# `w_down` by Strassen's seven block products, with weight blocks summed by accumulating DMAs

## The chip, the cores and the metric

The kernel runs on one core of one Trainium2 chip. The core has TensorE (PE), VectorE (DVE), ScalarE (ACT) and GpSimd (POOL), each with a queue of its own that runs in order, and 16 DMA engines; SyncE (SP) issues the transfers. The metric is the device time of one execution in microseconds; the median of three timed runs is shown.

## The reference

One decoder layer over 512 tokens of width 1024 in float32: token mixing (sparse attention beside dilated attention), cross-attention into 256 memory tokens, and the MLP that the change is about:

```python
hm = rmsnorm(x, norm_mlp_g[l])
x = x + jnp.square(jax.nn.relu(hm @ w_up[l])) @ w_down[l]      # w_up 1024 x 4096, w_down 4096 x 1024
return rmsnorm(x, norm_final_g)
```

## The kernel before

Every dense product is done in three passes. A float32 operand is split into `hi`, its value rounded to the type `float32r`, and `lo`, the rest; `mm3` (line 155) issues for each chunk of 128 contracted rows the matmuls hi x hi, hi x lo and lo x hi. All matmuls are issued in line 107. One has a stationary block of 128x128 and moves 512 columns through it.

Weights come in units of two chunks, [128, 2, 512] or 512 KB. `load_weight` (line 132) loads a unit with SP into `wraw` (three buffers), ACT rounds it into `whi` (line 129), and POOL or DVE subtracts to give `wlo` (line 130). `whi` and `wlo` have six buffers each. A string such as "vppp" says for the four units of a load who subtracts: v is DVE, p is POOL.

The MLP is a loop over four quarters `g` of 1024 hidden features (line 782). In each quarter `up_groups` computes the hidden features transposed, features on partitions and 512 tokens in columns, in eight groups of 24 matmuls. `evac_up` takes a group out of its PSUM bank (three banks `mm`): ACT applies relu, DVE squares, ACT rounds to hi and DVE subtracts to lo (lines 800 to 804). Then `project_add` (line 579) multiplies by the quarter's 1024 rows of `w_down`: for two halves of 512 columns and four tiles of 128 tokens, eight chunks by three matmuls; DVE multiplies the bank by the row's 1/rms squared (`r_mlp2`) and adds it to the residual `xr` (line 596). In the last quarter `finish` follows each addition: the row's square sum, 1/rms on POOL, the final gain (half on POOL, line 770), and the stores.

A planner in the compiler orders the instructions of each engine by a simulated time line. While `ordered[0]` is true, PE's instructions keep the order of the program; in the MLP this ends after the first `w_up` half. Tiles of one tag share buffers, and a writer waits for the last reader of the buffer it takes.

Of the kernel before, what the change touches and what calls it, by code (L numbers as in the profile page):

```python
# [17 lines left out]
P = 128  # L18
# [46 lines left out]
def kernel(  # L65
# [89 lines left out]
    def mm3(dst, a, b, first=True, last=True, ks=None):  # L155
        """dst += sum_k a_k^T b_k, a and b as (hi list, lo list); lo x lo is below float32."""
        n = len(a[0])
        for k in ks if ks is not None else range(n):
            mmul(dst, a[0][k], b[0][k], start=first and k == 0, stop=False)
            mmul(dst, a[0][k], b[1][k], start=False, stop=False)  # L160
            mmul(dst, a[1][k], b[0][k], start=False, stop=last and k == n - 1)
# [40 lines left out]
    def transpose_half(rows, g0, his, los, bank=bank_tp):  # L202
        """rows [128 tokens, 4 chunks of 128] -> transposed, times the gain, as hi + lo per chunk."""
# [11 lines left out]
    # =============================== token mixing ===============================  # L215
    p1a, p1b = ExitStack(), ExitStack()
# [267 lines left out]
    def keys_a():  # L484
        """Group A's keys and values from the latents."""
        p1a.close()
        res = state["res"] = ctx.enter_context(tc.tile_pool(name="res", bufs=1, reuse_waits="tile"))
        uv_raw = mtile([P, NH, DH], F32, "wraw", 3)
# [25 lines left out]
        vA = state["vA"] = [res.tile([P, 2, 512], F32, name=f"vA{c}") for c in "ab"]  # L514
# [34 lines left out]
    # dense products, attention and top-k in turns, so that each engine has work from another  # L549
# [21 lines left out]
    p1b.close()  # L571

    p2 = ctx.enter_context(tc.tile_pool(name="tmp2", bufs=1, reuse_waits="tile"))

# [32 lines left out]
    def up_groups(ms, wt, rhs, evac):  # L607
        """Weight-stationary groups: a new phase starts on the K chunks that are whole first."""
# [23 lines left out]
    def half_square(i, t, c0=0, c1=512):  # L632
        """What columns c0..c1 of half i of token tile t add to the row's mean square."""
# [35 lines left out]
    # =============================== cross-attention ===============================  # L669
# [19 lines left out]
    def cross_probs(h):  # L689
        """Head h's softmax over the memory tokens, transposed: per half of the queries (hi, lo)."""  # L690
# [66 lines left out]
    # =============================== squared-ReLU MLP ===============================  # L757
# [5 lines left out]
    r_mlp2 = p2.tile([P, NT], F32, name="r_mlp2")  # L763
    nc.vector.tensor_tensor(r_mlp2, r_mlp, r_mlp, op=ALU.mult)

    def finish(i, t, c0=0, c1=512):
        half_square(i, t, c0, c1)
        lo = xr[t][:, 0:512]
        if i == 0:
            nc.gpsimd.tensor_tensor(lo, lo, g_fin[0], op=ALU.mult)  # L770
# [5 lines left out]
        hi = xr[t][:, 512:]  # L776
        nc.scalar.activation(lo, lo, AF.Copy, scale=r)
        nc.sync.dma_start(out_rows[:, t, 0:512], lo)
        nc.vector.scalar_tensor_tensor(hi, hi, r, g_fin[1], op0=ALU.mult, op1=ALU.mult)
        nc.sync.dma_start(out_rows[:, t, 512:], hi)  # L780

    for g in range(4):
        if g % 2 == 0:
            hh = mtile([P, KD, S], F32R, "h0")
            hl = [mtile([P, 4, S], F32R, f"u2{c}") for c in "ab"]
            hid_hi = [hh[:, k, :] for k in range(KD)]
            hid_lo = [hl[k // 4][:, k % 4, :] for k in range(KD)]
        else:
            hh = [mtile([P, 2, S], F32R, f"ghi{i}") for i in range(4)]
            hl = [mtile([P, 2, S], F32R, f"glo{i}") for i in range(4)]  # L790
            hid_hi = [hh[k // 2][:, k % 2, :] for k in range(KD)]
            hid_lo = [hl[k // 2][:, k % 2, :] for k in range(KD)]
        for i in range(2):
# [15 lines left out]
        def hid(t):  # L809
            tsl = slice(t * P, (t + 1) * P)  # L810
            return [a[:, tsl] for a in hid_hi], [a[:, tsl] for a in hid_lo]

        project_add(w_down[0], 8 * g, hid, finish if g == 3 else None, "vppp", scale=r_mlp2, last=g == 3)


# [27 lines left out]
```

## Time and profile before

| what | value |
|---|---|
| timed runs | 846.23, 846.34, 846.51 us; median 846.34 |
| profiled execution, first to last instruction (span) | 843.6 us |
| median beyond that span | 2.7 us |
| PE busy | 821.7 us, 97% |
| DVE, ACT, POOL busy | 474.4 (56%), 331.4 (39%), 293.2 us (35%) |
| granted PE clock, mean | 0.992 |
| moved by DMA | 77.34 MB, 92 GB/s |

The profile has no other time of the profiled execution than its span, from the first to the last instruction; the timed runs also hold what lies around that. Busy time of PE is that of pipelined matmuls, so the distance from one matmul to the next is read from counts in a stretch and not from the length of one.

### The profile page before, as it was taken

The numbers are of one execution on the slowest core, as the hardware profiler recorded it, in microseconds if no ns is written. First come the engines' busy times: TensorE is split into PE (matmuls) and PEld (weight loads), VectorE is DVE, ScalarE is ACT, GpSimd is POOL, SyncE is SP. The second block draws the span as 40 slices with busy tenths as digits, with TensorE's granted clock in tenths as the row PEclk, the third lists the DMA queues.
The fourth block names the chain that finished last, engine by engine and source line by source line (L and its number), as shares of the span: only waits on it lengthen the run. The fifth ranks groups of instructions, "written<-read, shape, count | busy, mean of one in ns | idle before, by whom it ended". The sixth has DMA issues, their size and how long they took to land.

```text
span 843.6 us, 11086 instructions
## 1 busy us (share of the span) xinstructions
PE 821.7 (97%) x4182; PEld 679.2 (81%) x4182; DVE 474.4 (56%) x1010; ACT 331.4 (39%) x676; POOL 293.2 (35%) x179
## 2 busy tenths in 40 slices
PE   7899999999999999999999999999999999999997
PEld 6788787886787788788898878888888888888886
DVE  7876999998777634535673344423542244225413
ACT  5354424457754524223464433213431243123322
POOL 5734303131513405544501233333333333333351
PEclk9899999999999999999999999999999999999999
DMA  7443122112412303332510223333233322322202
GB/s 278 125 125 88 33 74 70 63 21 80 150 53 99 96 5 100 99 100 86 184 56 19 82 100 101 101 99 100 100 100 99 100 100 97 103 91 85 99 1 100
DMA packets 44516, 77.34 MB, mean 92 GB/s; under 512 B 4752, under 2 KB 10544, under 8 KB 44464
## 3 DMA queue, kind: packets, MB, share of 16 engines
q1 hardware_dynamic: 44464, 76.64, 27.8%
q8 instruction: 33, 0.54, 0.3%
q14 instruction: 19, 0.16, 0.1%
HBM read 74.01 MB, written 2.10 MB: 90 GB/s over the span
## 4 chain that ended last, share of the span: by engine, by line
PE 85%; DVE 11%; issue 1%; POOL 1%; ACT 1%; DMA 0%; SPq 0%; POOLq 0%; ACTq 0%; DVEq 0%
PE mm L107 71%; PE tp L112 5%; PE sc L107 5%; PE pv L107 4%; DVE m L525 1%; DVE ghi L360 1%; DVE tok L279 1%; DVE glo L526 1%; DVE rb L271 1%; DVE tok L271 1%; DVE whi L127 1%; DVE wlo L130 1%; DVE ghi L526 1%; DMA u2a<-in_x_dram 0%; DVE ghi L358 0%
## 5 line engine op out<-in xcount | busy, mean ns | idle before, releaser
L130 POOL TENSOR_TENSOR wlo<-wraw,whi 128x1024 fp32r<-128x1024 f32 (+2 forms) x107 | 256.2, 2408 | 404.5 <-ACT whi L129 318.8
L107 PE MATMUL mm<-whi,h 128*128 128x512 f32 (+2 forms) x624 | 200.1, 381 | 3.9 <-DVE h L213 2.0
L129 ACT CAST whi<-wraw 128x1024 fp32r<-128x1024 f32 (+3 forms) x111 | 114.3, 1030 | 149.6 <-PE mm L107 105.4
L107 PE MATMUL mm<-h,whi 128*128 128x512 f32 (+1 forms) x448 | 154.9, 369 | 0.0
L107 PE MATMUL mm<-wlo,h 128*128 128x512 f32 (+2 forms) x376 | 141.9, 379 | 0.2 <-DVE wlo L130 0.2
L107 PEld LDWEIGHTS mm<-whi,h 128*128 128x128 f32 x624 | 117.9, 195 | 22.0 <-ACT whi L129 2.2
L107 PE MATMUL mm<-u,whi 128*128 128x512 f32 x320 | 124.7, 390 | 0.0
L107 PE MATMUL mm<-u,wlo 128*128 128x512 f32 x320 | 123.5, 389 | 0.0
L107 PE MATMUL mm<-whi,ghi 128*128 128x512 f32 (+1 forms) x264 | 102.0, 390 | 0.0
L107 PE MATMUL mm<-whi,glo 128*128 128x512 f32 (+1 forms) x264 | 101.5, 385 | 0.0
L107 PE MATMUL mm<-wlo,ghi 128*128 128x512 f32 (+1 forms) x264 | 100.7, 383 | 0.0
L107 PEld LDWEIGHTS mm<-h,whi 128*128 128x128 f32 x448 | 81.1, 188 | 14.3 <-issue 1.0
L130 DVE TENSOR_TENSOR wlo<-wraw,whi 128x1024 fp32r<-128x1024 f32 (+2 forms) x24 | 62.2, 2591 | 37.5 <-ACT whi L129 37.5
L107 PEld LDWEIGHTS mm<-wlo,h 128*128 128x128 f32 x376 | 72.6, 194 | 11.1 <-DVE wlo L130 0.6
L107 PEld LDWEIGHTS mm<-u,whi 128*128 128x128 f32 x320 | 60.1, 188 | 12.4
L107 PEld LDWEIGHTS mm<-u,wlo 128*128 128x128 f32 x320 | 60.0, 188 | 12.5
L802 DVE TENSOR_TENSOR sq<-r 128x512 f32<-128x512 f32 x32 | 22.0, 689 | 66.7 <-ACT r L800 66.7
L107 PEld LDWEIGHTS mm<-whi,glo 128*128 128x128 f32 x264 | 49.6, 188 | 10.1 <-issue 0.2
L107 PEld LDWEIGHTS mm<-wlo,ghi 128*128 128x128 f32 x264 | 49.7, 188 | 9.6 <-issue 0.4
L107 PEld LDWEIGHTS mm<-whi,ghi 128*128 128x128 f32 x264 | 49.6, 188 | 9.4 <-issue 0.2
L409 ACT ACTIVATE p<-p,mx 128x128 f32<-128x128 f32 (+3 forms) x64 | 35.8, 560 | 29.4 <-DVE mx L407 28.5
L800 ACT ACTIVATE r<-mm 128x512 f32<-128x512 f32 x32 | 19.1, 598 | 64.8 <-PE mm L107 64.8
(212 smaller groups left out, 1116.7 us busy)
## 6 DMA issues: line engine op xcount, KB each, us to landing
wraw<-in_w_up_dram SPq DMA_DIRECT2D x32, 512.0 KB, 3.8
wraw<-in_w_down_dram SPq DMA_DIRECT2D x32, 512.0 KB, 3.6
wraw<-in_w_in_dram SPq DMA_DIRECT2D x16, 512.0 KB, 3.6
wraw<-in_w_kv_cross_dram SPq DMA_DIRECT2D x16, 512.0 KB, 3.9
wraw<-in_w_out_dram SPq DMA_DIRECT2D x8, 512.0 KB, 3.6
wraw<-in_w_q_cross_dram SPq DMA_DIRECT2D x8, 512.0 KB, 3.6
wraw<-in_w_o_cross_dram SPq DMA_DIRECT2D x8, 512.0 KB, 4.1
wraw<-in_w_in_dram SPq DMA_DIRECT2D x8, 256.0 KB, 2.9
```

Of the source, the lines that this page charges most:

```text
L107: ins = nc.tensor.matmul(*a, **k)
L112: ins = nc.tensor.transpose(*a, **k)
L127: nc.vector.tensor_copy(hi, raw)
L129: nc.scalar.copy(hi, raw)
L130: (nc.gpsimd if how in "pP" else nc.vector).tensor_tensor(lo, raw, f32(hi), op=ALU.subtract)
L271: nc.vector.scalar_tensor_tensor(o, i, r, tab, op0=ALU.mult, op1=ALU.mult)
L279: nc.vector.tensor_tensor(dst[:, :, c, :], ra[:, :, c, :], rbv[:, :, c, :], op=ALU.add)
L360: nc.vector.scalar_tensor_tensor(acc[b], rl[:, :n], wh, acc[b], op0=ALU.mult, op1=ALU.add)
L409: nc.scalar.activation(pr[:, c], pr[:, c], AF.Exp, bias=mx[:, i:i + 1], scale=-1.0, accum_out=sm[:, i:i + 1])
L526: nc.vector.match_replace(acc[b], m8, acc[b], GONE)
L800: nc.scalar.activation(r, ps, AF.Relu)
L802: nc.vector.tensor_tensor(sq, r, r, op=ALU.mult)
```

## The change

Each quarter's product with `w_down` (512 tokens x 1024 features by 1024 x 1024) is seen as 2 x 2 blocks: tokens in halves of 256, features in even and odd chunks of 128, output columns in halves of 512. Seven block products instead of eight are formed by Winograd's variant of Strassen's scheme, each of two token tiles by four chunks by three matmuls. Three kinds of sums belong to it:

- Sums of hidden blocks, `s` with four slots, are made in `evac_up` from each pair of an even and an odd chunk: four DVE operations of 256 columns, one ACT rounding, one subtraction on POOL (on DVE for the last pair).
- Sums of weight blocks are made by DMA: a tile `xw` is loaded with block (1, 0) and POOL then issues transfers with `accum_op=ALU.add` that add blocks (1, 512), (2, 512) and (2, 0) one after the other; after each step the tile is split. One product uses the sum of two blocks loaded in the same way into `wraw`.
- Products are added to or subtracted from the four blocks of `xr`, by DVE from the bank, or by an ACT copy and POOL additions. Two banks (`keep`) gather products 1, 7 and 4 over the quarter, two others (`five`) products 5 and 6.

The row's 1/rms is now multiplied in before the square: `row_scale` transposes it once on PE, and the evacuation is max(ps, 0) x rT on DVE and the square on ACT. `finish` takes the halves of a row in either order. Group A's values `vA` get a pool of their own which is closed before the pool of the later stages is opened. `ordered` stays true through the MLP. Besides, comments are gone.

```diff
+    def weight_pair(w, rows, c0, how, plus=None):
+        raw = mtile([P, 2, 512], F32, "wraw", 3)
+        nc.sync.dma_start(raw, rows(w)[:, :, c0:c0 + 512])
+        if plus is not None:
+            prows, p0 = plus
+            nc.gpsimd.dma_start(raw, prows(w)[:, :, p0:p0 + 512], accum_op=ALU.add)
+        return split_pair(raw, how)
+
+    def split_pair(raw, how):
+        hi = mtile([P, 2, 512], F32R, "whi", 6)
+        lo = mtile([P, 2, 512], F32R, "wlo", 6)
+        split_unit(raw, hi, lo, how)
+        return hi, lo
...
-    r_mlp2 = p2.tile([P, NT], F32, name="r_mlp2")
-    nc.vector.tensor_tensor(r_mlp2, r_mlp, r_mlp, op=ALU.mult)
+    def row_scale():
+        tp = bank_tp()
+        for t in range(NT):
+            tpose(tp[:, t * P:(t + 1) * P], r_mlp[:, t:t + 1].to_broadcast([P, P]), ident)
+        rT = p2.tile([P, S], F32, name="rT")
+        nc.scalar.copy(rT, tp)
+        rows_ready.append(rT)
...
             def evac_up(m, ps, i=i):
+                if not rows_ready:
+                    row_scale()
                 c = 4 * i + m
+                q, odd = c // 2, c % 2
-                nc.scalar.activation(r, ps, AF.Relu)
+                nc.vector.scalar_tensor_tensor(r, ps, 0.0, rows_ready[0], op0=ALU.max, op1=ALU.mult)
-                nc.vector.tensor_tensor(sq, r, r, op=ALU.mult)
-                nc.scalar.copy(hid_hi[c], sq)
-                nc.vector.tensor_tensor(hid_lo[c], sq, f32(hid_hi[c]), op=ALU.subtract)
+                nc.scalar.activation(sq, r, AF.Square)
+                ring[odd] = sq
+                part, src = (slice(1, 3), sq) if odd else (slice(0, 1), sq[:, 0:256])
...
+                nc.scalar.copy(hi, src)
+                nc.vector.tensor_tensor(lo, src, f32(hi), op=ALU.subtract)
+                if not odd:
+                    return
...
+                s = p2.tile([P, 4, 256], F32, name=nm("S"), tag="S", bufs=1)
+                nc.vector.tensor_tensor(s[:, 0], a22, a21, op=ALU.subtract)
+                nc.vector.scalar_tensor_tensor(s[:, 1], s[:, 0], -1.0, a11, op0=ALU.mult, op1=ALU.subtract)
+                nc.vector.tensor_tensor(s[:, 2], a11, a21, op=ALU.subtract)
+                nc.vector.scalar_tensor_tensor(s[:, 3], s[:, 1], -1.0, a12, op0=ALU.mult, op1=ALU.subtract)
+                nc.scalar.copy(s_hi[q], s)
+                (nc.gpsimd if q < 3 else nc.vector).tensor_tensor(s_lo[q], s, f32(s_hi[q]), op=ALU.subtract)
 
             up_groups(list(range(4)), wt, hm, evac_up)
-            ordered[0] = False
...
-        project_add(w_down[0], 8 * g, hid, finish if g == 3 else None, "vppp", scale=r_mlp2, last=g == 3)
+        xw = mtile([P, 2, 2, 512], F32, "u2b")
+        def sums(step):
+            row, col = ((1, 0), (1, 512), (2, 512), (2, 0))[step]
+            out = []
+            for u in range(2):
+                src = unit_rows(g, row, u)(w)[:, :, col:col + 512]
+                if step == 0:
+                    nc.sync.dma_start(xw[:, u], src)
+                else:
+                    nc.gpsimd.dma_start(xw[:, u], src, accum_op=ALU.add)
+                out.append(split_pair(xw[:, u], "p"))
+            return out
...
+        wts = sums(0)
+        for t in range(2):
+            product(keep[t], t, of_a(0), wts)
+            p1 = p2.tile([P, 512], F32, name=nm("p1"), tag="pc", bufs=2)
+            nc.scalar.copy(p1, keep[t])
+            add(t, left, p1, eng=nc.gpsimd)
+        wts = block(2, 0, "vp")
+        for t in range(2):
+            ps = bank_mm()
+            product(ps, t, of_a(1), wts)
+            add(t, left, ps)
+            done(0, t)
+        wts = sums(1)
+        five = [bank_tp() for _ in range(2)]
+        for t in range(2):
+            product(five[t], t, of_s(1), wts)
+            add(t + 2, right, five[t], ALU.subtract)
+        wts = block(2, 512, "vp")
+        for t in range(2):
+            product(five[t], t, of_s(4), wts, first=False)
+            add(t, right, five[t], ALU.subtract)
+        wts = sums(2)
+        for t in range(2):
+            product(keep[t], t, of_s(2), wts, first=False)
+            u2 = p2.tile([P, 512], F32, name=nm("u2"), tag="pcT1", bufs=2)
+            nc.scalar.copy(u2, keep[t])
+            add(t, right, u2, ALU.subtract, nc.gpsimd)
+            add(t + 2, right, u2, ALU.subtract, nc.gpsimd)
+            done(1, t)
+        wts = block(1, 512, "vp", (2, 512))
+        for t in range(2):
+            ps = bank_mm()
+            product(ps, t, of_s(3), wts)
+            add(t + 2, left, ps)
+            add(t + 2, right, ps, ALU.subtract)
+            done(1, t + 2)
+        wts = sums(3)
+        for t in range(2):
+            cuts = (0, 512) if g < 3 or t == 0 else (0, 256, 512)
+            for c0, c1 in zip(cuts, cuts[1:]):
+                product(keep[t], t, of_a(2), wts, first=False, cut=slice(c0, c1))
+                add(t + 2, slice(c0, c1), keep[t][:, c0:c1])
+                done(0, t + 2, c0, c1)
```

## Rows read from the trace of the kernel before

**Rows 1.** Busy us (instructions) of each engine by stretch, MLP stage; last columns clock, DMA share, GB/s.
```profile
core 0: us, PE busy (x) PEld busy (x) DVE busy (x) ACT busy (x) POOL busy (x), PEclk, DMA share, GB/s
520.00:600.00 80.00, 80.00 (x354) 66.25 (x353) 30.21 (x25) 23.20 (x28) 27.11 (x11) 1.00 0.28 92
680.00:760.00 80.00, 80.00 (x354) 66.25 (x353) 31.88 (x26) 24.17 (x29) 29.49 (x12) 1.00 0.31 105
760.00:843.60 83.60, 77.35 (x364) 64.83 (x363) 29.82 (x33) 26.31 (x42) 28.72 (x23) 0.98 0.20 70
```

**Rows 2.** Chain that ended last, from 480 us: start us, us, what.
```profile
490.87 0.70 PE tp L112 x4
491.57 340.05 PE mm L107 x1500
...
831.64 0.76 DVE xr L596
...
832.49 0.73 ACT junk L642 x2
...
833.56 0.55 POOL rfin L182
...
839.07 0.75 DVE xr L779
```

**Rows 3.** Waits from 490 us: who <- for whom: us in total, times, longest.
```profile
POOL wlo L130 <- ACT whi L129: 202.9, 28, 12.7
ACT whi L129 <- PE mm L107: 84.8, 26, 13.4
```

**Rows 4.** The same for the queue of SP, which issues the loads.
```profile
SPq L145 <- POOL wlo L130: 235.0, 28, 14.7
```

**Rows 5.** Instructions of single lines: duration ns min/median/max, first and last start us, shapes.
```profile
L596 DVE SCALAR_TENSOR_TENSOR xr<-mm,r_mlp,xr x17: 479/750/752, 548.8 to 837.4; 128x512 f32<-128x512 f32 x15, 128x256 f32<-128x256 f32 x2
...
L800 ACT ACTIVATE r<-mm x32: 597/598/599, 499.8 to 793.6; 128x512 f32<-128x512 f32 x32
...
L802 DVE TENSOR_TENSOR sq<-r x32: 676/692/693, 500.4 to 796.6; 128x512 f32<-128x512 f32 x32
...
L804 DVE TENSOR_TENSOR u2b<-sq,h x8: 691/693/2486, 519.8 to 710.9; 128x512 fp32r<-128x512 f32 x8
...
L594 DVE TENSOR_TENSOR xr<-xr,mm x8: 671/683/689, 316.0 to 489.9; 128x512 f32<-128x512 f32 x8
...
L130 POOL TENSOR_TENSOR wlo<-wraw,whi x107: 1831/2397/2852, 11.2 to 815.4; 128x1024 fp32r<-128x1024 f32 x98, 128x768 fp32r<-128x768 f32 x8, 128x928 fp32r<-128x928 f32 x1
...
L130 DVE TENSOR_TENSOR wlo<-wraw,whi x24: 833/3118/3415, 8.1 to 793.3; 128x1024 fp32r<-128x1024 f32 x22, 128x928 fp32r<-128x928 f32 x1, 128x512 fp32r<-128x512 f32 x1
...
L770 POOL TENSOR_TENSOR xr<-xr,g_fin x2: 1292/1294/1297, 811.8 to 818.2; 128x512 f32<-128x512 f32 x2
...
L129 ACT CAST whi<-wraw x111: 624/1052/1057, 7.1 to 812.6; 128x1024 fp32r<-128x1024 f32 x100, 128x768 fp32r<-128x768 f32 x8, 128x928 fp32r<-128x928 f32 x2, 128x512 fp32r<-128x512 f32 x1
```

**Rows 6.** Timeline of SP's queue, two stores of a finished tile: start us, us, what.
```profile
826.59 0.36 SPq L778 DMA_DIRECT2D out_dram<-u3a  x1
827.00 0.42 SPq L780 DMA_DIRECT2D out_dram<-u3a  x1
```

**Rows 7.** DMA issues: what, queue, count, KB each, median us to landing.
```profile
wraw<-in_w_down_dram SPq DMA_DIRECT2D x32, 512.0 KB, 3.6
```

**Rows 8.** Timeline of DVE, three los beside POOL: start us, us, what, [idle before].
```profile
703.82 2.49 DVE L804 TENSOR_TENSOR u2b<-sq,h 128x512 fp32r<-128x512 f32 x1 [1.35 <-ACT h L803]
706.23 3.42 DVE L130 TENSOR_TENSOR wlo<-wraw,whi 128x1024 fp32r<-128x1024 f32 x1
...
728.05 3.12 DVE L130 TENSOR_TENSOR wlo<-wraw,whi 128x1024 fp32r<-128x1024 f32 x1 [4.46 <-ACT whi L129]
```

**Rows 9.** Timeline of POOL in the same stretches.
```profile
703.35 5.21 POOL L130 TENSOR_TENSOR wlo<-wraw,whi 128x1024 fp32r<-128x1024 f32 x2 [10.78 <-ACT whi L129]
...
725.34 4.75 POOL L130 TENSOR_TENSOR wlo<-wraw,whi 128x1024 fp32r<-128x1024 f32 x2 [11.02 <-ACT whi L129]
```

More of the change, by code (lines that the diff above doesn't have):

```diff
@@ L153, in load_weight, with mm3 @@
         return his, los
-    def mm3(dst, a, b, first=True, last=True, ks=None):
+    def weight_pair(w, rows, c0, how, plus=None):
[10 more added lines that the diff above has]
+        return hi, lo
+    def mm3(dst, a, b, first=True, last=True, ks=None, again=False):
         n = len(a[0])
         for k in ks if ks is not None else range(n):
-            mmul(dst, a[0][k], b[0][k], start=first and k == 0, stop=False)
-            mmul(dst, a[0][k], b[1][k], start=False, stop=False)
-            mmul(dst, a[1][k], b[0][k], start=False, stop=last and k == n - 1)
+            mmul(dst, a[0][k], b[0][k], start=first and k == 0, stop=False, skip_group_check=again)
+            mmul(dst, a[0][k], b[1][k], start=False, stop=False, skip_group_check=again)
+            mmul(dst, a[1][k], b[0][k], start=False, stop=last and k == n - 1, skip_group_check=again)
     mhalf = main.tile([P, 1], F32, name="mhalf")
@@ L213, in transpose_half @@
                 nc.vector.scalar_tensor_tensor(los[c], tps[i][:, j, :], g, f32(his[c]), op0=ALU.mult, op1=ALU.subtract)
-    p1a, p1b = ExitStack(), ExitStack()
+    p1a, p1b, va_pool = ExitStack(), ExitStack(), ExitStack()
     att = p1b.enter_context(tc.tile_pool(name="att", bufs=1, side="right"))
@@ L487, in keys_a @@
         res = state["res"] = ctx.enter_context(tc.tile_pool(name="res", bufs=1, reuse_waits="tile"))
+        own = va_pool.enter_context(tc.tile_pool(name="va", bufs=1, reuse_waits="tile"))
         uv_raw = mtile([P, NH, DH], F32, "wraw", 3)
@@ L513, in keys_a @@
         nc.sync.dma_start(kA_all[64:96, :, :], krT[64:96, None, :].to_broadcast([32, NH, S]))
-        vA = state["vA"] = [res.tile([P, 2, 512], F32, name=f"vA{c}") for c in "ab"]
+        vA = state["vA"] = [own.tile([P, 2, 512], F32, name=f"vA{c}") for c in "ab"]
         for t in range(NT):
@@ L571 @@
     p1b.close()
+    va_pool.close()
     p2 = ctx.enter_context(tc.tile_pool(name="tmp2", bufs=1, reuse_waits="tile"))
@@ L762 @@
         nc.sync.dma_start(g_fin[h], norm_final_g[:, 512 * h:512 * h + 512].to_broadcast([P, 512]))
-    r_mlp2 = p2.tile([P, NT], F32, name="r_mlp2")
-    nc.vector.tensor_tensor(r_mlp2, r_mlp, r_mlp, op=ALU.mult)
+    rows_ready = []
+    def row_scale():
[5 more added lines that the diff above has]
+        rows_ready.append(rT)
+    ended = {}
     def finish(i, t, c0=0, c1=512):
         half_square(i, t, c0, c1)
-        lo = xr[t][:, 0:512]
-        if i == 0:
-            nc.gpsimd.tensor_tensor(lo, lo, g_fin[0], op=ALU.mult)
+        part = xr[t][:, 512 * i:512 * i + 512]
+        if t not in ended:
+            nc.gpsimd.tensor_tensor(part, part, g_fin[i], op=ALU.mult)
+            ended[t] = i
             return
@@ L775, in finish, with unit_rows @@
         rstd_of(half_ss.pop(t), r)
[L776 to L780, printed above, removed]
-    for g in range(4):
[L783 to L792, printed above, removed]
+        first = xr[t][:, 512 * (1 - i):512 * (1 - i) + 512]
+        nc.scalar.activation(first, first, AF.Copy, scale=r)
+        nc.sync.dma_start(out_rows[:, t, 512 * (1 - i):512 * (1 - i) + 512], first)
+        nc.vector.scalar_tensor_tensor(part, part, r, g_fin[i], op0=ALU.mult, op1=ALU.mult)
+        nc.sync.dma_start(out_rows[:, t, 512 * i:512 * i + 512], part)
+    lo2 = p2.tile([P, 3, 256], F32R, name="lo2")
+    ring = {}
+    def unit_rows(g, row, u):
+        return lambda w: w[8 * P * g:8 * P * (g + 1), :].rearrange("(k q p) c -> p q k c", q=2, p=P)[:, row - 1, 2 * u:2 * u + 2]
+    for g in range(4):
+        big = mtile([P, 5, 3, 256], F32R, "h0")
+        two = mtile([P, 2, 3, 256], F32R, "u2a")
+        a_hi = [big[:, i] for i in range(4)]
+        a_lo = [two[:, 0], two[:, 1], lo2, big[:, 4]]
+        s_hi = [mtile([P, 4, 256], F32R, f"ghi{i}") for i in range(4)]
+        s_lo = [mtile([P, 4, 256], F32R, f"glo{i}") for i in range(4)]
         for i in range(2):
@@ new lines, in evac_up @@
+                ring[odd] = sq
+                part, src = (slice(1, 3), sq) if odd else (slice(0, 1), sq[:, 0:256])
+                hi = a_hi[q][:, part].rearrange("p s t -> p (s t)")
+                lo = a_lo[q][:, part].rearrange("p s t -> p (s t)")
+                nc.scalar.copy(hi, src)
+                nc.vector.tensor_tensor(lo, src, f32(hi), op=ALU.subtract)
+                if not odd:
+                    return
+                a11, a21 = ring[0][:, 0:256], ring[0][:, 256:]
+                a12, a22 = ring[1][:, 0:256], ring[1][:, 256:]
@@ new lines @@
+            up_groups(list(range(4)), wt, hm, evac_up)
+        xw = mtile([P, 2, 2, 512], F32, "u2b")
+        w = w_down[0]
+        def sums(step):
[9 more added lines that the diff above has]
+            return out
@@ new lines, in block, with product @@
+        def block(row, col, how, plus=None):
+            return [weight_pair(w, unit_rows(g, row, u), col, how[u],
+                                None if plus is None else (unit_rows(g, plus[0], u), plus[1])) for u in range(2)]
+        def product(dst, t, a, wts, first=True, cut=slice(0, 512)):
+            his, los = a
+            tsl = slice(t * P, (t + 1) * P)
+            mm3(dst[:, cut], ([h[:, tsl] for h in his], [l[:, tsl] for l in los]),
+                ([wts[k // 2][0][:, k % 2, cut] for k in range(4)], [wts[k // 2][1][:, k % 2, cut] for k in range(4)]),
+                first, again=True)
@@ new lines, in of_a, with of_s, add @@
+        def of_a(slot):
+            return [h[:, slot] for h in a_hi], [l[:, slot] for l in a_lo]
+        def of_s(n):
+            return [h[:, n - 1] for h in s_hi], [l[:, n - 1] for l in s_lo]
+        left, right = slice(0, 512), slice(512, D)
+        def add(t, half, src, op=ALU.add, eng=nc.vector):
+            dst = xr[t][:, half]
+            eng.tensor_tensor(dst, dst, src, op=op)
+        done = finish if g == 3 else lambda i, t, c0=0, c1=512: None
+        keep = [bank_s() for _ in range(2)]
```

2 lines of the change are left out of this document (removed).

## The prediction

> **What bounds the kernel now.** I read the engines' busy time by stretch first. The MLP (every matmul of `w_up` and `w_down`) lies between 491.6 us and the end. In each 80 us of it PE is busy for 80.00 us with 354 matmuls at a granted clock of 1.00, while DVE, ACT and POOL are busy for about 30, 23 and 27 us [rows 1]. The chain of waits says the same: one piece of 340.05 us is matmuls behind one another, 1500 of them [rows 2]. So a matmul of 512 columns costs 80.00 / 354 = 0.226 us of the end time, and whatever the others do is hidden. The list of waits shows why: POOL waits for ACT's rounding, ACT for PE to free a weight buffer [rows 3], SP's loads for POOL [rows 4]. Weights are ready early and stand before PE. What is taken off PE comes off the end, as long as the three others keep up; that is the question here.
>
> **What is removed.** A quarter of `w_down` (1024 hidden features) is 2 halves x 4 token tiles x 8 chunks x 3 = 192 matmuls. Seven products of 2 token tiles x 4 chunks x 3 = 24 make 168. Four quarters: 96 matmuls fewer, 96 x 0.226 = 21.7 us. PE's order is written out for the whole MLP (`ordered` stays true), so no planner can lose this count.
>
> **What is added on PE.** `row_scale` transposes four 128x128 tiles once; four such took 0.70 us [rows 2]: +0.7. Its copy stands before the first evacuations, but three `mm` banks and two more half groups (2 x 12 x 0.226 = 5.4 us) cover 0.6 us of ACT.
>
> **Evacuation.** The 1/rms is now in the first step (DVE, from the bank, like L596's 0.75 us), the square goes to ACT (like L800, 0.60), so a bank is freed by DVE 0.15 us later. A group of 24 matmuls lasts 5.4 us and there are three banks: nothing. If DVE were late by over 10 us, PE would wait.
>
> **DVE and ACT budgets.** A quarter now lasts 360 x 0.226 = 81.4 us. DVE gains 16 operations of 256 columns for S (0.44 each: L802's 0.69 scaled by L596's 0.48 to 0.75) = 7.0, one 1024-wide lo and one more weight lo (up to 3.4 each [rows 5]) = 6.8, and 12 adds of 0.69 for 8 of 0.75 = 2.3; 16 us more than about 30. ACT gains 6 weight roundings and 4 for S (10 x 1.05) and 4 copies of 0.6: 13 more than 24. Both stay under 60% and are hidden.
>
> **POOL's budget decides.** Today it does 12 weight los of 2.4 us a quarter. After: 6 (`w_up`) + 8 (`sums`) + 3 (`block`) = 17, 3 of S, 6 adds of 1.29 (like L770 [rows 5]) and 8 accumulating DMAs of d each: 20 x 2.4 + 7.7 + 8d = 55.7 + 8d of 81.4 us. That fits; its distribution is tight. Let T0 be the first matmul of product 1. A product is 24 x 0.226 = 5.4 us, seven are 38 us. There are 6 weight buffers (`whi`, `wlo`), 2 per product: a buffer is freed about 12 us before its next contents are needed, so POOL can't work ahead. Between T0-3 and T0+42, when the next `w_up` needs its fourth unit, POOL owes 9 los for the products, 3 for `w_up` (28.8 us), 6 adds (7.7) and 6 DMAs (those of `sums(1)` go before T0): 36.5 + 6d. DVE operations that share its reads push it: 3 weight los and the S chain, up to 7.8 us; half is 3.9. Demand 40.4 + 6d, room 44.7: POOL is late by 6d - 4.3.
>
> No DMA is issued from POOL in this trace, so d has ends only: SP's issue of a plain transfer, 0.36 to 0.42 us, and the whole way of 512 KB from issue to landing, 3.6 us [rows 6, 7]. These give no lateness and 17.3 us a quarter, 0 to 69 us in all. I take d = 1.0, an estimate: an issue is of the kind of the first row, and an accumulating one names its destination twice over 256 rows, hence some 2.5 times as much. Lateness 1.7 x 4 quarters = +6.8 us. (The last quarter has no `w_up` behind it, -7.2 us, but four multiplications by the final gain, 4 x 1.29 = 5.2, on the same queue.)
>
> The Trainium skill ("DMA: Bandwidth & Descriptors", Latency and other measured facts) gives a first byte after about 1 us for such DMAs, put down to descriptor emission on POOL's cores, against 0.6 us for SP's. No row here shows it; by it d would be about 1 too, and the sum the same.
>
> **Waits queued on POOL.** An accumulating DMA waits for its tile's previous split, or for SP's load; behind it stand los of the next units and the adds of product 7. Product 3's DVE adds to the same `xr` columns wait for these adds, and `mm` banks behind them; at 1.7 us that is inside the two spare banks.
>
> **DMA.** Bytes for `w_down` double (8 blocks of 1 MB a quarter for 4), 12 MB in 81 us for 8 in 87; the 16 engines were busy 0.28 to 0.31 of the time [rows 1], so 0.30 x 1.6 = 0.48, and with the reading of the destinations, 4 MB more, 0.65. The chain of one `xw` half per step is landing + rounding 1.05 + lo 2.4. `sums(2)` can be issued at about T0+6, once product 5's units are split (buffers free at T0, one rounding, two los); with landing L, `sums(3)` follows at 13 + L (rounding, two los, an issue) and its second lo ends at 16.4 + 2L; product 4 needs it at T0+32.6. So L may be 8.1 us, over twice the plain 3.6: no cost taken.
>
> **Tail and the rest.** The end chain (add, square sum, POOL's power, scaling, store; [rows 2]) is the same with halves swapped: 0. Reusing the memory of `vA` makes the first tiles of the last pool wait for group A's last products, behind which `keys_cross` keeps PE busy: 0.
>
> **Sum**, against the profiled execution: span 843.6 - 21.7 + 0.7 + 6.8 = 829.4 us. The median of the timed runs is 846.3, 2.7 us above that span; the same 2.7 gives 832.1, so 832.
>
> **Rivals.**
> 1. *POOL's queue is the bound (the other side).* If an accumulating DMA costs POOL more than d = 1.6, the lateness 6d - 4.3 exceeds (21.7 - 0.7) / 4 = 5.3 us a quarter and the change loses. At d = 2.2: 8.9 x 4 = 35.6, so 846.3 - 21.0 + 35.6 = 861. For it: no row caps d below 3.6, and the queue is in order. Against: POOL is at 33% now, and an SP issue takes 0.4.
> 2. *DVE behind POOL's reads.* The rows show it: of 512-column los, median 0.69, the one that began inside a POOL lo took 2.49, ending with it; the next took 3.42, and another one 3.12 [rows 5, 8, 9]; the last ended 1.1 us after POOL. After T0, the last hidden chunk goes through DVE 0.75, ACT 0.6 + 0.6, DVE lo, four S operations, ACT 1.05 and DVE's `s_lo`, which product 5's twelfth matmul needs at T0 + 10.9 + 11 x 0.226 = 13.4. If POOL has no gap, six of these wait out a POOL lo each and the last adds its 1.1: 3.0 + 6 x 2.4 + 1.1 = 18.5, 5.1 us late, x 4 = 20.4: 846.3 - 21.0 + 20.4 = 846, no change. For it: POOL's demand after T0. Against: while it issues DMAs (4 us) and waits for landings it reads nothing, and DVE then does several in a row. Behind it stands the Trainium skill ("SBUF — State Buffer", Who interferes with whom): a DVE instruction with two SBUF inputs contends with a POOL instruction that reads SBUF, and the second to issue is blocked to the end of the first. By this rule the trace agrees (2.49 for 0.69), and the sum would be 846.
> 3. *Accumulation is slow.* If a landing takes L over 8.1 us, each further us costs 2 a quarter. At L = 14 (four plain ones): 11.8 x 4 = 47, so 872. Break-even at 8.1 + 5.3 / 2 = 10.8. For it: the destination must be read too. Against: the 16 engines are idle 70% of the time.
>
> **Chances.** Forecast (lateness 0 to 4.3 us a quarter, so 825 to 842): 0.60. Rival 1: 0.17. Rival 2: 0.13, of which 0.05 still faster, 0.05 same, 0.03 slower. Rival 3: 0.10. A measurement of this kernel tells 0.2% (1.7 us) from no change. Faster 0.65, same 0.05, slower 0.30. The likeliest case's own range is 825 to 842; with rivals 1 and 2 the range is 825 (no lateness: 846.3 - 21.0) to 861, leaving out rival 3 and the far end of 1.
>
> **What would show it.** Right: about 96 matmuls fewer; in each 80 us of the MLP PE busy over 76, clock 1.00; POOL 75 to 85% busy in the `w_down` stretches; accumulating DMAs landing within 8 us; PE's few gaps in front of products 6, 7, 3 or 4, ended by POOL's lo. Rival 1: the same gaps with POOL at 100%, and 2 us or more between its instructions around each DMA. Rival 2: gaps before product 5 ended by DVE's `s_lo`. Rival 3: ACT's rounding of `xw` waiting for a DMA, POOL idle. The prediction is wrong if POOL is late by over 5 us a quarter, or if PE's clock falls below 1.00 after such gaps, which no row prices.

## The result, and the profile after

The changed kernel takes 873.2 us (four runs, 871.2 to 876.3) where the kernel before takes 846.4 (four runs): a ratio of 1.0315 (95% interval 1.0292 to 1.0338). The forecast was 832 and its range ended at 861, so both sign and size were wrong. The profiled execution took 871.23 us with a span of 869.5.

The profile of the kernel after, its parts on busy time, queues (packets, MB, share of 16 engines' span) and DMA issues (last column: median us from issue to landing), and the line of one issuing instruction (duration ns min/median/max), show what the change was to do, and what it cost:

```profile
PE 813.1 (94%) x4078; PEld 667.5 (77%) x4078; DVE 553.2 (64%) x1097; ACT 376.4 (43%) x733; POOL 446.5 (51%) x267
...
q0 software_dynamic: 8704, 16.78, 12.0%
...
wraw<-in_w_down_dram SPq DMA_DIRECT2D x24, 512.0 KB, 4.8
u2b<-in_w_down_dram POOLq DMA_DIRECT2D x24, 512.0 KB, 6.5
...
wraw<-in_w_down_dram POOLq DMA_DIRECT2D x8, 512.0 KB, 6.4
...
L881 POOL DMA_DIRECT2D u2b<-in_w_down_dram x24: 1176/1208/2153, 525.5 to 842.6; - x24
```

The queue `q0` is new. It holds the 32 accumulating transfers, and a median one keeps POOL for 1.21 us (`u2b` is the memory of `xw`) and lands 6.4 to 6.5 us after its issue; SP's loads of `w_down` beside them went from 3.6 [rows 7] to 4.8.

By stretch, the MLP stage of the kernel after (columns as in [rows 1]):

```profile
520.00:600.00 80.00, 71.97 (x300) 58.53 (x299) 44.77 (x45) 30.80 (x38) 57.33 (x31) 0.94 0.60 145
600.00:680.00 80.00, 71.34 (x306) 58.25 (x305) 46.35 (x41) 31.73 (x39) 64.06 (x33) 0.96 0.57 134
627.00:676.00 49.00, 40.34 (x169) 32.58 (x168) 26.64 (x21) 16.34 (x19) 40.74 (x23) 0.93 0.64 144
...
636.00:642.00 6.00, 5.66 (x25) 4.64 (x26) 4.26 (x6) 4.38 (x5) 4.90 (x4) 1.00 1.08 189
642.00:647.00 5.00, 5.00 (x24) 4.14 (x23) 0.69 (x1) 0.00 (x0) 1.61 (x1) 1.00 0.95 257
```

Where 354 matmuls ran in 80 us, about 303 do now: PE has gaps in the MLP for the first time. POOL is at 72 to 80%, in the `w_down` stretch of a quarter (627 to 676) at 83%: busy, not full. The last two lines matter most. Over 80 us the 16 DMA engines are busy 0.57 to 0.60 of the time, a little under the 0.65 worked out beforehand; in the eleven microseconds from 636 they are busy all of it (a share can pass 1, as a packet's whole time is counted where it starts).

What PE waits for from 490 us in the kernel after (us in total, times, longest):

```profile
PE tp L107 <- DVE xr L906: 23.5, 4, 7.6
...
PE mm L107 <- DVE h L854: 3.2, 3, 1.1
...
PE sc L107 <- DVE xr L906: 3.1, 1, 3.1
PE sc L107 <- DVE h L854: 3.1, 1, 3.1
```

Four waits, one a quarter, make 23.5 us, and they are for an addition on DVE (L906), not for a weight. All the waits shown, 32.9 us, are for DVE; the one that is left out here for POOL is 0.9 us. The chain of waits through the second quarter's gap tells why (start us, us, what):

```profile
633.23 1.19 POOL u2b L881
...
635.99 10.93 DMA u2b<-in_w_down_dram
...
647.97 1.05 ACT whi L129
...
649.04 5.70 DVE wlo L130
654.74 0.61 DVE xr L906
...
655.40 4.72 PE tp L107 x12
```

Read it backwards. Product 6's second token tile starts at 655.40, because it gathers in the bank that product 5's addition has to read first. That addition could have run from about 645.1, when product 5 was over (647.79 less product 6's first tile, 12 x 0.227), but in DVE's queue it stands behind a subtraction for product 3's first weight unit, a product that comes two later. That subtraction waited for ACT's rounding, and the rounding, whose own transfer was issued at 635.24 and so had landed by 642.1 (the longest of its kind took 6.8 us), stood in ACT's queue behind that of `xw`, which waited for an accumulating DMA that took 10.93 us. So a late transfer whose result PE did not need yet stopped PE through two queues that run in order. The timelines of ACT, of DVE and of POOL in the kernel after show the pieces:

```profile
647.02 1.05 ACT L129 CAST whi<-u2b 128x1024 fp32r<-128x1024 f32 x1 [5.98 <-DMA u2b<-in_w_down_dram]
647.97 1.04 ACT L129 CAST whi<-wraw 128x1024 fp32r<-128x1024 f32 x1
```
```profile
642.39 0.69 DVE L906 TENSOR_TENSOR xr<-xr,tp 128x512 f32<-128x512 f32 x1 [0.41 <-PE tp L107]
649.04 5.70 DVE L130 TENSOR_TENSOR wlo<-wraw,whi 128x1024 fp32r<-128x1024 f32 x1 [5.96 <-ACT whi L129]
```
```profile
633.23 1.19 POOL L881 DMA_DIRECT2D u2b<-in_w_down_dram  x1
...
635.24 1.65 POOL L162 DMA_DIRECT2D wraw<-in_w_down_dram  x1
635.99 2.14 POOL L881 DMA_DIRECT2D u2b<-in_w_down_dram  x1
...
648.56 5.09 POOL L130 TENSOR_TENSOR wlo<-u2b,whi 128x1024 fp32r<-128x1024 f32 x2
```

DVE idles 5.96 us, then its subtraction takes 5.70 us instead of a median 1.226: it began inside two subtractions of POOL and ended 1.1 us after them, the pattern of [rows 8, 9]. PE stopped at 655.40 - 7.61 = 647.79. Of the gap of 7.61 us, 5.70 - 1.23 = 4.5 are this blocking; the other 3.1 would have gone, by this sum, had the transfer landed in 7.8 us instead of 10.93. POOL had issued three accumulating transfers within 3 us while the DMA engines were full.

The gap also costs clock. PE's timeline in the kernel after, from the end of the gap, and the stretches there (the granted clock is the third number from the right):

```profile
655.40 0.80 PE L107 MATMUL tp<-whi,ghi 128*128 128x512 f32 x1 [7.61 <-DVE xr L906]
655.99 0.63 PE L107 MATMUL tp<-wlo,ghi 128*128 128x512 f32 x1
656.41 0.63 PE L107 MATMUL tp<-whi,glo 128*128 128x512 f32 x1
...
```
```profile
655.00:659.00 4.00, 3.60 (x9) 2.87 (x10) 0.94 (x2) 0.00 (x0) 3.37 (x2) 0.50 0.88 156
...
662.00:669.00 7.00, 7.00 (x32) 5.82 (x31) 0.68 (x2) 3.99 (x5) 6.97 (x6) 1.00 0.40 73
```

For some 3.6 us the granted clock is 0.50, the lower of the two levels (1.2 GHz), and matmuls follow each other at 0.43 us, not 0.227. Eight of them cost 8 x 0.20 = 1.6 us more after this gap. Over the whole MLP 52 matmuls stand 0.3 to 0.9 us behind the one before, most of them after a gap, and together they take some 10 us over 0.226 each. With PE's waits that accounts for most of the 45.9 us by which the four quarters exceed their matmuls (below).

### The profile page after: what moved, and what is told of

Its sections match the earlier page's. It is cut to its first block, busy times and chain, and to the rows that moved or that the text cites. A ratio compares the mean times of both kernels' runs of the same rounds, so it can differ in the third digit from the quotient of the medians.

```text
span 869.5 us, 11165 instructions
## 1 busy us (share of the span) xinstructions
PE 813.1 (94%) x4078; PEld 667.5 (77%) x4078; DVE 553.2 (64%) x1097; ACT 376.4 (43%) x733; POOL 446.5 (51%) x267
## 3 DMA queue, kind: packets, MB, share of 16 engines
q0 software_dynamic: 8704, 16.78, 12.0%
## 4 chain that ended last, share of the span: by engine, by line
PE 72%; DVE 15%; POOL 5%; DMA 4%; issue 2%; ACT 2%; SPq 0%; POOLq 0%; ACTq 0%
PE mm L107 51%; PE sc L107 9%; PE tp L112 5%; PE pv L107 4%; DVE wlo L130 3%; DMA u2b<-in_w_down_dram 3%; PE tp L107 3%; POOL wlo L130 3%; DVE m L543 1%; DVE ghi L377 1%; DVE tok L296 1%; ACT whi L129 1%; DVE glo L544 1%; DVE rb L288 1%; DVE tok L288 1%
## 5 line engine op out<-in xcount | busy, mean ns | idle before, releaser
L130 POOL TENSOR_TENSOR wlo<-wraw,whi 128x1024 fp32r<-128x1024 f32 (+2 forms) x95 | 229.3, 2426 | 234.0 <-ACT whi L129 149.7
L107 PE MATMUL mm<-whi,h 128*128 128x512 f32 (+2 forms) x536 | 166.0, 380 | 7.6 <-DVE h L854 3.2
L107 PE MATMUL mm<-wlo,h 128*128 128x512 f32 (+2 forms) x280 | 104.5, 375 | 0.0
L130 POOL TENSOR_TENSOR wlo<-u2b,whi 128x1024 fp32r<-128x1024 f32 x32 | 81.3, 2596 | 9.5 <-ACT whi L129 9.5
L107 PE MATMUL mm<-whi,ghi 128*128 128x512 f32 x160 | 64.3, 402 | 0.0
L107 PE MATMUL mm<-whi,glo 128*128 128x512 f32 x160 | 62.9, 393 | 0.0
L107 PE MATMUL mm<-wlo,ghi 128*128 128x512 f32 x160 | 62.5, 390 | 0.0
L129 ACT CAST whi<-u2b 128x1024 fp32r<-128x1024 f32 x32 | 33.5, 1051 | 41.8 <-DMA u2b<-in_w_down_dram 32.5
L107 PE MATMUL tp<-whi,ghi 128*128 128x512 f32 x64 | 28.5, 446 | 23.5 <-DVE xr L906 23.5
L865 POOL TENSOR_TENSOR glo<-S,ghi 128x1024 fp32r<-128x1024 f32 x12 | 28.8, 2402 | 36.5 <-ACT ghi L864 25.2
```

The lines of the kernel that those rows point to most:

```text
L107: ins = nc.tensor.matmul(*a, **k)
L865: (nc.gpsimd if q < 3 else nc.vector).tensor_tensor(s_lo[q], s, f32(s_hi[q]), op=ALU.subtract)
```

## The experiments

All times are medians; the ratio is to the kernel before, run beside it on the same chip (its medians there: 845.8 to 847.0 us). A quarter is timed in the profiled execution, from its first matmul with `w_up` to that of the next quarter (the last one to the end of its product 4); 360 matmuls alone would be 81.4 us. The changed kernel's four quarters took 91.9, 92.7, 92.3 and 94.6 us, 371.5 in all, where the matmuls need 325.6. An expectation that did not come true is named as such.

**e1: only the 1/rms moved into the evacuation, `w_down` by eight products.**

```diff
-                nc.scalar.activation(r, ps, AF.Relu)
+                nc.vector.scalar_tensor_tensor(r, ps, 0.0, rows_ready[0], op0=ALU.max, op1=ALU.mult)
-                nc.vector.tensor_tensor(sq, r, r, op=ALU.mult)
+                nc.scalar.activation(sq, r, AF.Square)
```

> The kernel before with one part of the change alone: 1/rms multiplied in ahead of the square (DVE evacuates, ACT squares, four transposes more). Theory A (this part costs nothing but the transposes, and the whole loss lies in the w_down products): 846.4 + 0.7 = 847, PE busy throughout the MLP. Rival (the evacuation through DVE holds banks back and is part of the loss): over 850.

846.75 against 847.02, ratio 1.0002 (0.9993 to 1.0012), as theory A says. This part is innocent.

**e2: the DVE subtraction of product 3's first unit kept behind the additions.**

```diff
+            if eng is nc.vector:
+                tc.keep_in_program_order(ins)
...
-        wts = block(1, 512, "vp", (2, 512))
+        wts = block(1, 512, "op", (2, 512))     # "o": on DVE, in program order
```

> The changed kernel; only the order in DVE's queue differs: the subtraction that makes the low part of product 3's first weight unit stands behind the additions that empty the two banks of products 5 and 6, not ahead of the second of them. Theory A (these additions stood behind that subtraction, which waits for an accumulating DMA two engines away, and PE waited for the bank): the gap before the second tile of product 6 goes (5.1, 7.8, 7.5 and 3.8 us, with some 1.5 us each at half clock, about 30 us), and lateness of the sums themselves takes some of it back, about 4 us a quarter: 857, within 850 to 862. Theory B (the chain of accumulating DMAs sets the pace, whatever stands ahead of the addition; PE only waits elsewhere): 868 to 875, with new gaps before products 7 and 4.

876.27, ratio 1.0352 (1.0330 to 1.0375): not better, against theory A and just above theory B's range. But the quarters are 90.9, 89.0, 89.3 and 107.6. The gap before product 6 is gone from three quarters and they gain only 1.0 to 3.7 us each; the last loses 13. In DVE's timeline of this kernel the kept subtraction now stands behind the last quarter's scaling by the final 1/rms, which waits for POOL:

```profile
844.17 1.75 DVE L812 SCALAR_TENSOR_TENSOR u3a<-u3a,rfin,g_fin 128x512 f32<-128x512 f32 x1 [12.95 <-POOL rfin L201]
...
850.60 3.36 DVE L130 TENSOR_TENSOR wlo<-wraw,whi 128x1024 fp32r<-128x1024 f32 x1
```

**e9: the same order in the first three quarters only** (`"op" if g < 3 else "vp"`).

> The changed kernel with the order in DVE's queue fixed in the first three quarters only (in the run with all four the last quarter lost 13.7 us, because that subtraction then also stood behind the scaling by the final 1/rms). Theory B' (both count: the order costs what the first three quarters of that run showed, 1.0, 3.7 and 3.0 us, and the chain of accumulating DMAs the rest): 873 - 8 = 865, within 862 to 868. Theory B (the chain alone): 871 to 875. Theory A (the order alone): 850.

869.85, ratio 1.0267 (1.0245 to 1.0288); quarters 91.3, 91.1, 89.5, 98.0. The total lies between the two ranges expected: with the order mended where it can be, 3.4 of 27 us come back. (In this execution the last quarter, whose subtraction is left as it was, is some 3.5 us longer; why stays open.) PE's waits of this kernel name what is late next, POOL's weight subtractions for products 7 and 4, which gather in the `sc` banks:

```profile
PE sc L107 <- POOL wlo L130: 12.5, 9, 4.0
PE tp L107 <- DVE xr L908: 5.1, 1, 5.1
```

The order is how the lateness reached PE first; it is not what makes things late.

**e3: all 32 accumulating transfers as plain loads by SP, nothing summed.**

```diff
-            nc.gpsimd.dma_start(raw, prows(w)[:, :, p0:p0 + 512], accum_op=ALU.add)
+            nc.sync.dma_start(raw, prows(w)[:, :, p0:p0 + 512])
-                    nc.gpsimd.dma_start(xw[:, u], src, accum_op=ALU.add)
+                    nc.sync.dma_start(xw[:, u], src)
```

> The changed kernel, with each accumulating DMA of POOL replaced by a plain load of the same bytes by SP (the weight blocks are not summed, so part of the computation is left out). Theory A and B (what is late comes from the accumulating DMAs): 826 to 835. Rival C (POOL's subtractions, the port that it shares with DVE, or the order of the hidden sums set the pace by themselves): over 845, with PE gaps ended by subtractions and no DMA in the chain.

836.28, ratio 0.9878 (0.9864 to 0.9893), just above the 826 to 835 expected and far from the rival's 845. By stretch, the last line a short one behind PE's first wait:

```profile
520.00:600.00 80.00, 76.89 (x331) 62.88 (x330) 41.79 (x50) 36.98 (x46) 54.46 (x25) 0.98 0.45 147
600.00:680.00 80.00, 79.68 (x349) 64.95 (x349) 47.21 (x49) 34.55 (x44) 56.23 (x26) 1.00 0.48 154
680.00:760.00 80.00, 79.99 (x352) 65.58 (x351) 45.97 (x50) 35.35 (x44) 57.20 (x26) 1.00 0.50 158
...
540.00:544.00 4.00, 4.00 (x12) 3.13 (x12) 3.54 (x4) 1.39 (x3) 2.12 (x2) 0.62 0.85 265
```

The same bytes arrive, and every engine has the same work save POOL's 32 issues; the order on DVE is also that of the changed kernel, and PE is nearly full again. So 36.9 us of the changed kernel hang on these transfers. What stays above 846.3 - 21.0 = 825.3 is 11 us, of which 6.9 are two waits of PE: 3.1 for DVE's `h` in the first quarter's product 1, and 3.8 for an `xr` addition. The other 4.1 are matmuls that follow each other late: by the count made above, 25 of them take 4.2 us over 0.226 each. Nine stand behind the first wait at the lower clock: from 540 to 544 PE, never idle, gets through 12 matmuls at a granted clock of 0.62 where 4.00 / 0.226 = 17.7 would fit. Why the others come late stays open.

**e4: the transfers issued by POOL but plain** (`accum_op` dropped in both lines), **and e5: that with the order of e2.**

> The changed kernel, with the accumulating DMAs still issued by POOL but without accumulation (the weight blocks are not summed). If the doubled time of an accumulating transfer on the 16 engines (0.188 us a packet for 0.098) is what makes the chain late: landing falls from 6.5 to about 4.5 us and the time to about 845 (838 to 852). If issuing them from POOL (1.2 us each in POOL's queue, and the waits there) is what costs: 865 or more, as the changed kernel.

> The changed kernel with both edits of the second and the fourth run: POOL's transfers without accumulation (the weight blocks are not summed), and the low part of product 3's first weight unit behind the additions in DVE's queue. Theory B (the accumulating chain set the pace, so that the order in DVE's queue could not show; with faster transfers the order is what is left): the gaps before the second tile of product 6 (2.1, 3.7 and 3.9 us, each with 1 to 1.5 us at half clock) go, 857 - 13 = 844, within 840 to 850. Rival (the order never matters, PE waits for the same los a product later): 853 to 860.

e4: 857.19, ratio 1.0119 (1.0091 to 1.0146), between the two ranges expected. Lines of its issues (duration ns min/median/max), its landings and the same subtraction in DVE's timeline; last, that subtraction in e3 and the first of the two POOL subtractions that it met there:

```profile
L881 POOL DMA_DIRECT2D u2b<-in_w_down_dram x24: 722/722/959, 526.7 to 830.2; - x24
```
```profile
u2b<-in_w_down_dram POOLq DMA_DIRECT2D x24, 512.0 KB, 4.1
```
```profile
642.10 5.83 DVE L130 TENSOR_TENSOR wlo<-wraw,whi 128x1024 fp32r<-128x1024 f32 x1 [1.80 <-ACT whi L129]
647.86 0.68 DVE L906 TENSOR_TENSOR xr<-xr,tp 128x512 f32<-128x512 f32 x1
```
```profile
636.43 2.23 DVE L130 TENSOR_TENSOR wlo<-wraw,whi 128x1024 fp32r<-128x1024 f32 x1 [1.80 <-ACT whi L129]
```
```profile
635.18 2.40 POOL L130 TENSOR_TENSOR wlo<-u2b,whi 128x1024 fp32r<-128x1024 f32 x1
```

A landing of 4.1 us for `xw` is as short as SP's in e3 (4.5), and still 20.9 us are lost against e3. POOL's queue is later by its issues (0.72 us each), its pair of subtractions slides onto DVE's, and that is held 5.83 us, over both, where in e3 it was held over one of them (2.23). e5 bears this out: 856.17 in all, the rival's figure, ratio 1.0120 (1.0102 to 1.0137), but its first three quarters are 83.5, 84.4 and 85.3 where e4's are 88.4, 88.9 and 88.3; its last is 103.3, the trap of e2. So 12.4 us of e4's loss, of the 15.7 that these three quarters lose against e3 (84.8, 82.3 and 82.9), are DVE's queue, in quarters where it can be mended.

**e13: accumulating transfers of half the columns** (in both lines), hence the same count of packets at half the bytes.

```diff
-                    nc.gpsimd.dma_start(xw[:, u], src, accum_op=ALU.add)
+                    nc.gpsimd.dma_start(xw[:, u, :, 0:256], src[:, :, 0:256], accum_op=ALU.add)
```

> The changed kernel, each accumulating DMA moves half of the columns (the other half is not summed): as many issues on POOL, half of the time on the 16 engines. If transfer and landing make the chain late: landing 6.5 falls to about 4.5 us, as in the run with plain transfers from POOL, and the time to 857 (852 to 861). If the issue on POOL does (1.2 us an accumulating one for 0.72 a plain one, waits in its queue): 866 or more.

863.60, ratio 1.0199 (1.0180 to 1.0218), again between the two ranges. The issue keeps its length, the landing falls to nearly that of e4:

```profile
L881 POOL DMA_DIRECT2D u2b<-in_w_down_dram x24: 1186/1302/2153, 525.3 to 835.0; - x24
```
```profile
u2b<-in_w_down_dram POOLq DMA_DIRECT2D x24, 256.0 KB, 4.4
```

So of the 16.0 us between e4 and the changed kernel, 9.6 go with the moving of the other half of the bytes, and 6.4 with what half the bytes leave, the longer issue among it.

These steps depend on DVE's order. The first three quarters together, in us, from one profiled execution each (the fourth holds the trap of e2):

| DVE's order | plain by SP | plain by POOL | accumulating by POOL |
|---|---|---|---|
| of the changed kernel | 249.9 (e3) | 265.6 (e4) | 276.9 |
| mended | not run | 253.2 (e5) | 272.0 (e9) |

In the changed kernel's order the issue from POOL costs 15.7 and accumulating 11.3 more; with the order mended, 3.3 (against e3) and 18.8. Mending the order frees plain transfers of most of their loss, and accumulating ones of little (4.9 of 27.0).

**e11: only product 3's two-block sum accumulates (8 transfers); e12: only the `xw` sums (24).**

> The changed kernel; only the two-block sum of product 3 is made by accumulating DMAs (8 of them), the other 24 transfers are plain loads by SP (those blocks are not summed). Theory of the chain (each of the three sums that follow one another on one tile waits for the split of the one before it, so these are late; a sum that can be prefetched is hidden): 836 to 841, as with plain loads. Rival (each accumulating DMA costs alike, 37 us over 32 of them): 845.

> The complement: the 24 transfers of the chain accumulate, product 3's second block is a plain load by SP (not summed). Theory of the chain: 865 to 873, nearly all of the loss. Rival (all alike): 864 or less, 836 + 28.

e11: 845.97, ratio 1.0004 (0.9992 to 1.0016). e12: 855.19, ratio 1.0105 (1.0090 to 1.0120). Both came out as the rival says, not as the theory of a late chain. Over e3 these are +9.7 and +18.9, together 28.6 of the 36.9: the missing 8.3 us appear only when both kinds are in flight. The chain on one tile is therefore not all of it: eight transfers that stand outside it cost 9.7. DVE in e11, at the same place of the second quarter:

```profile
643.03 1.22 DVE L130 TENSOR_TENSOR wlo<-wraw,whi 128x1024 fp32r<-128x1024 f32 x1 [2.01 <-ACT whi L129]
644.17 0.68 DVE L906 TENSOR_TENSOR xr<-xr,tp 128x512 f32<-128x512 f32 x1
```

The order is the same as in the changed kernel (subtraction, then addition) and does no harm in this quarter (82.1 us): the rounding came early enough, so that the subtraction took 1.22 us and not 5.70.

**e6: the sums by DVE additions, loads by SP; e7: that with three DVE subtractions of weights given to POOL.** Both compute all of the layer.

```diff
...
-                    nc.gpsimd.dma_start(xw[:, u], src, accum_op=ALU.add)
+                    nxt = mtile([P, 2, 512], F32, "wraw", WR)
+                    nc.sync.dma_start(nxt, src)
+                    nc.vector.tensor_tensor(xw[:, u], xw[:, u], nxt, op=ALU.add)
```

> The change with its weight sums made on DVE: SP loads each block into `wraw`, DVE adds it to the sum in SBUF; no DMA leaves POOL. The whole computation is done. Theory B: a step of the chain loses the 6.5 us landing and POOL its 8 x 1.2 us of issues, for 8 DVE additions of 1.25 us a quarter: 838 to 850. Rival (DVE behind POOL's reads: each of the 8 additions has two SBUF inputs and waits out a POOL subtraction of 2.4 us, and the evacuations queue up behind them): 855 to 870.

> As the run before, and the three subtractions a quarter that DVE made for the plain blocks go to POOL. If DVE's queue is the limit there: faster than the run before by 3 to 10 us. If POOL's queue is: slower by as much (POOL has 3 x 2.4 us a quarter more to do).

e6: 879.57, ratio 1.0396 (1.0374 to 1.0419), beyond both ranges. e7: 897.29, ratio 1.0602 (1.0586 to 1.0618). The group of e6's additions on DVE and PE's waits of e6:

```profile
L886 DVE TENSOR_TENSOR u2b<-u2b,wraw 128x1024 f32<-128x1024 f32 x24 | 37.2, 1550 | 17.7 <-DMA wraw<-in_w_down_dram 14.6 <-POOL wlo L131 1.3 <-POOL u3b L911 1.2
```
```profile
PE tp L108 <- DVE xr L911: 17.0, 8, 3.9
PE sc L108 <- DVE h L857: 14.1, 4, 4.8
```

Taking the sums off the DMA moves the loss to DVE's queue, and giving its work to POOL is worse by 17.7, more than the 3 to 10 expected: neither has room in the `w_down` stretch.

**e8: the sums made in DRAM by POOL's accumulating transfers during attention, the MLP loading them by SP; e10: the same spread over 16 places, with e9's order.** Both compute all of the layer.

```diff
+            d = dram.tile([P, 4, 512], F32, name=f"ws{g}{part}")
+            nc.gpsimd.dma_start(d[0:1, 0, 0:4], f32(tok))      # waits for a tile of attention
+            nc.gpsimd.dma_start(d, wblock(g, *terms[0]) if part in (0, 3) else summed[g, part - 1])
+            nc.gpsimd.dma_start(d, wblock(g, *terms[-1]), accum_op=ALU.add)
...
+                nc.sync.dma_start(raw, summed[g, part][:, 2 * u:2 * u + 2])
```

> The change with the weight sums made early: POOL's accumulating DMAs sum the blocks in DRAM while the attention runs (16 sums of 1 MB, two behind each block of queries), and the MLP loads finished sums by SP like any weight. The whole computation is done. Theory B (only the place of the accumulating DMAs in the MLP's chain is dear): as with plain loads, 836, within 830 to 842, first 490 us unchanged. Rival (the 16 DMA engines or POOL's queue are not free enough in the attention): the MLP starts later than at 492 us, by as much as the total is over 836.

> The sums made early in DRAM as in the run before, spread over 16 places from the attention to the end of the cross-attention, each addition issued one place behind its copy, and the order in DVE's queue fixed in the first three quarters. If theory B' holds and the early stages have room: MLP from 492 us, quarters of 84, 82.5, 82.5 and 88 us, end at 829 + 6.2 + 1.7 = 837, within 833 to 843, faster than the kernel before. If the 16 DMA engines are what is missing in the early stages: MLP starts after 497 us again and the total is 845 or more.

e8: 854.02, ratio 1.0097 (1.0080 to 1.0114). e10: 859.18, ratio 1.0149 (1.0124 to 1.0174). The forecasts of 836 and 837 failed. The MLP of e8, to its last matmul, lasts 343.3 us, 2.7 less than before, but starts at 501.7 instead of 491.3. An attention stretch of the kernel before, then of e8:

```profile
200.00:300.00 100.00, 100.00 (x657) 76.43 (x656) 71.65 (x207) 56.42 (x141) 34.05 (x14) 1.00 0.28 90
```
```profile
200.00:300.00 100.00, 96.65 (x620) 73.23 (x619) 78.04 (x200) 55.18 (x140) 51.16 (x39) 0.98 0.91 243
```

The DMA share rises from 0.28 to 0.91 and PE does 620 matmuls for 657. So the sums are paid in the attention instead, and spreading them did not help; which engine holds the attention up was not tested. No kernel here that computes the whole layer this way beats the kernel before.

## Why the prediction was wrong

Three terms of the sum failed: those for the transfers and for DVE, which were put at nothing, and that for POOL's lateness, put at 6.8 us. Together they measured 873.2 - 825.3 = 47.9.

- **Right.** The count: 104 records fewer on PE (4182 before, 4078 after), where 96 matmuls less and 4 transposes more make 92; about 12 records are missing from the trace. The transposes and 1/rms cost nothing that e1 can tell. POOL's share: 63.7 of 81.4, or 78%, worked out, 75 to 85% named for the `w_down` stretches; 72 to 80% and 83% measured, and not full, so rival 1 is not what happened. The issue d: 1.0 taken, 1.21 measured; the factor of 2.5 behind it rested on no row, so that nearness is luck. The first of `sums(2)`: at T0 + 6 worked out, at 633.23 with T0 = 627.16 measured in the second quarter. The DMA share: up to 0.65 worked out, 0.57 to 0.60 measured. PE's long gaps: product 6 was among the places named, but DVE's addition ends them, not POOL's subtraction. That the clock falls after gaps was named as unpriced; it took some 10 us in all.
- **The first step that failed is "DMA ... no cost taken", with L up to 8.1 us.** Accumulating instead of plain transfers from POOL cost 16.0 us in all (e4), 18.8 in three quarters where DVE's order is mended (e5, e9). The median landing, 6.5, is inside that bound, but the one that counted took 10.93, about rival 3's break-even of 10.8. The working used a mean load of 0.65 in place of the burst: three accumulating issues within 3 us, beside SP's loads, fill the engines (share 0.95 to 1.08 from 636 to 647). The bound also looked at one need alone. It asked when product 4 would miss its weights, and in e9 PE does stop inside product 4 for POOL's subtraction, up to 4.0 us at once. In the changed kernel PE stopped earlier, at product 6, for a bank whose reader stood on DVE behind a subtraction that no one needed yet.
- **"Both stay under 60% and are hidden", of DVE and ACT, failed with it.** Both shares came true (DVE 56 and 58%, ACT 38 and 40%), but DVE is not hidden: of the changed kernel's waits of PE 32.9 us are for DVE, and in e3, with no transfer from POOL, still 6.9. A share says nothing about what stands behind a waiting instruction. The working listed what is queued behind POOL's waits and not what is queued behind ACT's and DVE's. Rival 2 had the right blocking (POOL's pair held DVE 5.70 us here, 5.83 in e4) at another place: before product 5, by `s_lo`. The hold is not of one length: in e3 the subtraction at this place ended 1.1 us after the first of POOL's two, in the changed kernel and in e4 1.1 us after the second. The Trainium skill's rule for it ("SBUF — State Buffer", Who interferes with whom) is that the second to issue is blocked until the first is over. The hold in e3 agrees (2.23 us for 1.22); the hold over both subtractions is longer than the rule by itself gives.
- **The lateness term, +6.8, was mis-sized because its formula counts POOL's time alone.** With the measured issues 6d - 4.3 gives no lateness for plain ones (d = 0.72) and 3.0 us a quarter, 12 in all, for accumulating ones (d = 1.21). Measured were 20.9 us for plain issues (e4 over e3) and 6.4 more for accumulating ones at half the bytes (e13). POOL had the time; what the issues shifted is when its pairs of subtractions meet DVE's. The runs show that for 12.4 us (e4 against e5); for the rest it is argued.

In numbers, from 825.3 (the forecast without any lateness): +11.0 for sums and evacuation on DVE, ACT and POOL (e3), +20.9 for issuing from POOL (e4), +6.4 for accumulating at half the bytes (e13), +9.6 for the other half of the bytes: 873.2. The runs carry the steps in this order; with DVE's order mended they share the loss differently, as the table shows. That e13's step is the issue and not the packets, whose count is the same as in the changed kernel and nearly twice e4's, is not separated. Of e3's 11.0 us, 6.9 are waits for DVE and about 4 are matmuls that follow late, of which only those behind the first wait are explained.

Rival 3's figure, 872, came near by luck: it stands for a landing of 14 us in every step, and the median was 6.5. Its sign is there all the same: ACT's rounding of `xw` waits 32.5 us for the transfers, in nine waits, where in e3 it is 14.0 in seven. Its 2 us per us of landing beyond 8.1 would give 5.7 us a quarter at 10.93; that PE lost 5.9 a quarter to its one long wait (23.5 / 4) is another route to a like number.

## What to carry to other kernels

When a change makes a weight arrive later, don't ask only when PE needs that weight: for each engine that handles it (rounding, subtraction), list what stands behind it in that engine's queue, above all the instruction that frees a PSUM bank. A share of 0.6 on the DMA engines hides bursts at 1.0, and the landing to plan with is that of the worst transfer of a burst. And saved matmuls are worth their time only if their replacement fits into the stretch in which they were saved: 21 us of PE were bought here with transfers that cost 37 and sums that cost 11.

## What the runs showed of the hardware

- An accumulating transfer of 512 KB into `xw` keeps POOL 1.21 us at issue, a plain one from POOL 0.72 (e4), SP's issue takes 0.37. Its landing is 6.5 us in the median and 10.9 in a burst, that of plain ones from POOL 4.1. The queue's packets took 12.0% of 16 engines' span for 16.78 MB accumulating, 5.9% plain.
- After the gap of 7.6 us, PE ran for some 3.6 us at its lower level although it had been at 1.00 before.
- A DVE subtraction that met two POOL subtractions back to back was held over both in the changed kernel and in e4 (5.70 and 5.83 us for 1.22), over one in e3 (2.23).
